# A two-block transformer kernel: one activation table set for Exp and Ln, new rates for the modulation halves, head-norm squares in bursts of four

## The chip, the cores and the metric

The kernel runs on one core of a Trainium2 chip. The metric is the device time of one execution in microseconds (us), as the median of several runs. The engines are named TensorE (PE, with its weight loads PEld), VectorE (DVE), ScalarE (ACT), GpSimd (POOL) and SyncE (SP, which issues the loads here).

## The reference

Two transformer blocks work on 256 tokens of 2048 features, all in float32. The first mixes with eight stick-breaking heads and eight chunk-band heads; the second is modulated by a vector c and mixes with latent attention and sliding-window heads, then runs a gated feed-forward with a short convolution. Cut to what the change touches:

```python
def stick_breaking_attention(q, k, v):
    z = einsum('bhtd,bhsd->bhts', qb, kb) * scale
    log_stay = where(causal, log_sigmoid(-z), 0.0)
    after = cumsum(log_stay, axis=3, reverse=True) - log_stay
    w = where(causal, exp(log_sigmoid(z) + after), 0.0)
    ...

def chunk_band_attention(q, k, v, q_gain, k_gain, rel_table):
    q = rms_norm(q, q_gain)
    k = rms_norm(k, k_gain)
    ...

def second_block(x, c, w_ada, b_ada, ...):
    c_act = silu(c)
    mod = (c_act @ w_ada + b_ada)            # 2048 x 12288
    sh1, sc1, gt1, sh2, sc2, gt2 = split(mod, 6, axis=-1)
    h = rms_norm_2(x, g_pre_mix) * (1.0 + sc1) + sh1
    ...
```

## The kernel before

Every weight comes in chunks of 128 x 1024 float32 (512 KB). A class `Stream` (from L48) holds the list of chunks and takes each through three stages: its load into one of five `raw` buffers, issued on SyncE (L77); its split into an exact high part `whi` on ScalarE (L93) and a low part `wlo` on VectorE (L94), which runs up to three chunks ahead; and its products on TensorE, three for each run of 128 columns (`wmm`, L216 to L218, with the weights stationary; `xmm`, L233 to L235, with the activations stationary and the tokens on the partitions of the result). One chunk has 24 products of 256 columns or 12 of 512.

Tasks are Python generators. `Stream.tick` moves them on twice a chunk, once before it and once in its middle; what a task yields is the number of ticks until its next piece. So one tick is half a chunk. The order of the instructions on TensorE and SyncE is the order in which the code lists them. On VectorE, ScalarE and GpSimd a scheduler orders them by its own estimates; each engine then executes its queue strictly in that order.

The modulation `c_act @ w_ada` is a matrix-vector product and runs on VectorE. It has 192 halves; each loads 512 KB through the same five `raw` buffers and multiplies them with the replicated c (`crep`) in one instruction with an accumulated sum (`ada_half`, L330). `S.after_chunk = ada_tick` adds a rate to an accumulator after each listed chunk and lists a half whenever it has reached one, as long as fewer than a given number exist; `ada_rate(r, upto)` sets both. The halves have deadlines in the code: 64 of them (shift and scale) before the operand of block 2 is made (`make_u` from `start_u`), 160 before that of the feed-forward, 192 before the down projection.

The order of the work in block 1: 9 chunks of the first gates, 24 chunks of gate tiles (`gate_handler`, Silu on ScalarE), then `chunk_group(0)` and `chunk_group(1)`, each q, k and v of four chunk-band heads in 8 chunks apiece, then 16 chunks of values for the stick heads, then 32 chunks of q and k of the eight stick heads, then the 32 chunks of the output projection (`seq`). After k of a group, `head_norm` (L581) squares q and k of four heads (L590, sixteen instructions, eight between two yields), takes the inverse root and multiplies q and k (L599). After v, four `chunk_head` tasks start 1, 6, 11 and 16 ticks later: transposes, `qkT` on ScalarE, scores (L627, L628), a softmax with Exp, transposes to `pT`, products with v (L395, L396). A `stick_head` (L660) multiplies q and k by the tokens' factor into `qkT` on VectorE (L663), starts its scores two ticks later (L666), applies Abs, Exp and Ln on ScalarE (L205 is the line of every ScalarE activation except the split), adds them into `sp` on VectorE (L677), sums over keys on TensorE, and takes another Exp.

In block 2, sliding-window heads and latent heads use Exp, their gates Tanh; the feed-forward uses Silu. A compiler pass places a load of an activation table set in front of an activation whose function the loaded set lacks.

Of the kernel before, what the change touches and what calls it, by code (L numbers as in the profile page):

```python
# [12 lines left out]
AF = mybir.ActivationFunctionType  # L13
ALU = mybir.AluOpType

P = 128
T = 256
# [7 lines left out]
# columns of the packed vectors  # L25
# [9 lines left out]
# columns of the packed constants  # L35
# [12 lines left out]
class Stream:  # L48
    """The order of the work. Weight chunks go through three stages: their load, their split into exact high
    and low float32r parts, and their products; the first two run ahead of the third. Between the products  # L50
    of a chunk, tasks (generators that give the ticks to their next piece) are moved on."""

    RAW, AHEAD = (5,3)
# [9 lines left out]
    # -- the list of work  # L63
# [7 lines left out]
    # -- stages  # L71
# [27 lines left out]
    def split_ahead(self):  # L99
        """split until AHEAD chunks after the running one are ready"""  # L100
        w = sum(1 for i in range(self.nrun, self.nsplit) if self.items[i][0] == "w")
        while self.nsplit < len(self.items) and (w < self.AHEAD + 1 or self.items[self.nsplit][0] == "v"):
            if self.items[self.nsplit][0] == "w":
                w += 1
            self.split_one()

    def run(self):
        """runs every item listed so far"""
        while self.nrun < len(self.items):
            i = self.nrun  # L110
            if self.items[i][0] == "v":
                if self.nsplit <= i:
                    self.split_one()
                self.nrun += 1
                continue
            _, src, n, mms, pre, post = self.items[i]
            if pre is not None:
                pre()
            self.tick()
            self.split_ahead()  # L120
            hi, lo = self.parts.pop(i)
            fs = mms(hi, lo)
            h = (len(fs) + 1) // 2
            for f in fs[:h]:
                f()
            self.tick()
            for f in fs[h:]:
                f()
            self.nrun += 1
            if post is not None:  # L130
                post()

    # -- tasks
# [27 lines left out]
def two_blocks(ctx, tc, xT, cvec, cst, vecs, w1, wo1, bch, ada, wz, wv, wuq, wuk, wuv, bsw, wo2, wup, wup3, wdn, out):  # L161
# [42 lines left out]
    def act(**kw):  # L204
        nc.scalar.activation(**kw)  # L205
# [7 lines left out]
    def wmm(out, whi, wlo, a, first, last):  # L213
        """feature-major: out[feature, token] += W^T a"""
        ahi, alo = a
        mm(out, lhsT=whi, rhs=ahi, start=first, stop=False)  # L216
        mm(out, lhsT=whi, rhs=alo, start=False, stop=False)  # L217
        mm(out, lhsT=wlo, rhs=ahi, start=False, stop=last)  # L218

    def wchunk(lst):  # L220
        """lst: for each run of 128 columns: (out, operand, first, last), values or functions"""
        def mms(hi, lo):
            def one(c, e):
                out, a, first, last = e() if callable(e) else e
                wmm(out, hi[:, c * P:(c + 1) * P], lo[:, c * P:(c + 1) * P], a, first, last)
            return [lambda c=c, e=e: one(c, e) for c, e in enumerate(lst)]
        return mms

    def xmm(hi, lo, j, width, act2, out, b, first, last):
        """token-major: out += a^T W for a block of tokens"""  # L230
        w, t = slice(j * width, (j + 1) * width), slice(b * P, (b + 1) * P)
        ahi, alo = act2
        mm(out, lhsT=ahi[:, t], rhs=hi[:, w], start=first, stop=False)  # L233
        mm(out, lhsT=ahi[:, t], rhs=lo[:, w], start=False, stop=False)  # L234
        mm(out, lhsT=alo[:, t], rhs=hi[:, w], start=False, stop=last)  # L235

# [14 lines left out]
    def rsqrt_cols(v, n):  # L251
        """the same for a few single columns, 1/sqrt(v) / RS: y <- (v y^2 - 3 c^2) y leaves a factor -2 c^2 a step"""
        y = small.tile([P, 2], F32, tag="rz", name="rz", bufs=3)
        a = small.tile([P, 2], F32, tag="rb", name="rb", bufs=2)
        ts(out=y[:, :n].bitcast(I32), in0=v[:, :n].bitcast(I32), scalar1=-0.5, scalar2=1597463007.0, op0=ALU.mult,
           op1=ALU.add)
        for three in (3.0, 12.0, 768.0):
            for c in range(n):
                c1 = slice(c, c + 1)
                stt(out=a[:, c1], in0=y[:, c1], scalar=y[:, c1], in1=v[:, c1], op0=ALU.mult, op1=ALU.mult)  # L260
            for c in range(n):
                c1 = slice(c, c + 1)
                stt(out=y[:, c1], in0=a[:, c1], scalar=three, in1=y[:, c1], op0=ALU.subtract, op1=ALU.mult)
        return y[:, :n]

    def token_rstd(sqs, n):
        """sqs: tiles [P, 2, T] whose sum over tiles, halves and partitions is the sum of squares of each token;
        its mean's 1/sqrt, times 1 / RS"""
# [10 lines left out]
    def replicate(r, dst, gap=3, scale=RS):  # L279
        """dst[p, t] = scale * r of token t"""  # L280
# [17 lines left out]
    class SumSq:  # L298
        """running sum of squares over tiles [P, 2, T]; the last one stays apart"""
# [49 lines left out]
    def ada_rate(r, upto):  # L349
        """halves for each chunk from here on"""  # L350
        ada_acc[1:] = [r, upto]
    S.after_chunk = ada_tick

    # ---- softmax of scores in PSUM [P, 384]: 128 queries x 128 keys, 128 queries x 256 keys; the scores and
    # the biases come negated, so that the least is the negated maximum ----
# [42 lines left out]
    # =========================== block 1 ===========================  # L398
# [43 lines left out]
    def w_pair(srcs, acts, handler, n=16, per=8, tag="g"):  # L442
        """two tiles of 128 features share a bank; handler(bank) follows"""
# [27 lines left out]
    def x_group(srcs, acts, handler, tot, width, tag="g", apart=None):  # L471
        """width features of both blocks of tokens; handler(banks) follows. With apart, the first block is
        finished two chunks before the second, and apart(b, bank) follows each"""
# [42 lines left out]
    def gate_handler(j):  # L516
# [3 lines left out]
        def evac(ps):  # L520
            gt = p1.tile([P, 2, T], F32, tag="gate", name="gate", bufs=8)
            tt(out=gt, in0=two(ps), in1=rrep2, op=ALU.mult)
            act(out=gt, in_=gt, func=AF.Silu)
# [4 lines left out]
    # the first four tiles of gates go by k tiles, behind the split of x  # L528
# [21 lines left out]
    for j in range(2, 8):  # L550
        if j == 2:
            ada_rate(0.3, 96)
        w_pair(next_w1(4), hxs, gate_handler(j))
# [14 lines left out]
    # chunk-band heads  # L568
# [12 lines left out]
    def head_norm(qk, keys):  # L581
        """q, k of four heads, tokens on the partitions: times rsqrt of their mean squares"""
        ss = small.tile([P, 16], F32, tag="sst", name="sst", bufs=2)
        junk = p1.tile([P, 128], F32, tag="junk", name="junk", bufs=1)
        for w in range(2):
# [5 lines left out]
            yield 1  # L591
# [3 lines left out]
        for w in range(2):  # L595
# [4 lines left out]
            yield 1  # L600
# [51 lines left out]
    ada_rate(0.7, 96)  # L652
# [5 lines left out]
    # stick-breaking heads: scores with the keys on the partitions  # L658
# [36 lines left out]
    ada_rate(0.3, 96)  # L695
# [7 lines left out]
    # startup: the first chunks run behind the split of x  # L703
# [15 lines left out]
    # output projection; the residual; the next block's operand without its token factor  # L719
# [6 lines left out]
    def start_u():  # L726
        """room for x * gain, and the shift's columns beside it"""
# [40 lines left out]
    ada_rate(0.5, 96)  # L768
    for n, (j, a, hf) in enumerate(seq):
        if n == 20:  # L770
            ada_rate(0.0, 96)
# [11 lines left out]
    # =========================== block 2 ===========================  # L783
    def trick(srcs, tags, done):
        """some tiles of 128 features from the operand without its token factor: a few k tiles to a chunk"""
# [12 lines left out]
    def untrick(ps, dst, rr):  # L798
        """the token factor and the shift"""
# [7 lines left out]
    def form_h(pool_h, tmp, lst, rr, ish, nb, then=None):  # L807
        """x -> rms(x) * g * (1 + sc) + sh as high and low parts"""
# [38 lines left out]
    def split_q(src, sp=None, bufs=4):  # L847
        """two heads of 64 -> for each its high and low part, on the two halves of the partitions"""
# [60 lines left out]
    ada_rate(0.44, 160)  # L909
# [64 lines left out]
    # latents  # L974
# [71 lines left out]
    # latent attention, two heads at a time  # L1046
# [69 lines left out]
    ada_rate(0.2, 160)  # L1116
# [7 lines left out]
    # output projection, post-norm, gate, residual  # L1124
# [11 lines left out]
    def o_handler(j, a):  # L1136
        """squares and a copy of a pair of tiles; of the last pair each tile by itself"""
# [30 lines left out]
    # =========================== feed-forward ===========================  # L1168
# [35 lines left out]
    def conv_gate(i, z1, z2):  # L1204
        """the two halves of u before the convolution -> high and low parts of silu(u1) * u2"""
# [81 lines left out]
    # down projection: tokens on the partitions, as the output has them  # L1287
# [8 lines left out]
    def to_rows():  # L1296
        """gains along the free dimension, and x with tokens on the partitions"""
# [24 lines left out]
    def finish_block(b, ps):  # L1322
        """the last features, post-norm and residual of a block of tokens"""
# [32 lines left out]
# ---------------------------------------------------------------------------  # L1356
def _wunits(w, cols):
    """w [K, N] -> [len(cols), 128, K/128 * 128]: one unit for each run of 128 columns starting at cols"""
# [14 lines left out]
def _chunks(u):  # L1373
    """[U, 128, n * 1024] -> [U * n, 128, 1024]"""
# [4 lines left out]
def _several(w, cols):  # L1379
    """runs of 128 columns side by side, a few k tiles to a chunk"""  # L1380
# [117 lines left out]
```

## Time and profile before

| | before |
|---|---|
| median of 3 runs | 1987.45 us |
| lowest, highest run | 1982.82, 1987.96 us |
| span of the profiled execution, first to last instruction | 1973.9 us |
| own time of the profiled execution | not given apart from its span |
| TensorE matmul busy | 1912.1 us, 97% |
| TensorE weight load busy | 1792.9 us, 91% |
| VectorE busy | 1373.1 us, 70% |
| ScalarE busy | 1003.2 us, 51% |
| GpSimd busy | 255.7 us, 13% |
| read from HBM | 434.73 MB, 221 GB/s over the span |

The span leaves out what lies before the first and after the last instruction. Busy shares are averages over stages with different limits, so the views that matter are those of single stretches.

### The profile page before, as it was taken

What the parts mean: (1) busy time and instruction counts of PE and PEld (TensorE: products, weight loads), DVE (VectorE), ACT (ScalarE), POOL (GpSimd) and SP (SyncE); (2) the same over time, 40 slices, a digit from 0 to 9 for tenths busy, and PEclk for the clock granted to TensorE, in tenths of its full rate; (3) what the DMA queues carried; (4) which work ended last, traced back from release to release, by engine and by line L of the source; (5) the groups of instructions that cost most, each with busy time, mean ns of one, the idle gap of its engine ahead of it and who ended that gap; (6) DMA issues with size and microseconds to landing.
All of it is one profiled execution on the core that took longest, in us unless ns stands there. A gap on an engine that the chain in (4) does not pass through costs nothing. (4 is left out here: it accounts for less than half of the span.)

```text
span 1973.9 us, 35197 instructions
## 1 busy us (share of the span) xinstructions
PE 1912.1 (97%) x13844; PEld 1792.9 (91%) x13844; DVE 1373.1 (70%) x2204; ACT 1003.2 (51%) x1547; POOL 255.7 (13%) x327
## 2 busy tenths in 40 slices
PE   8998999999999999999999997999999999999997
PEld 7986878999998999999998997999999999988885
DVE  7667776666786666666778889987777766634444
ACT  6434544664465555554566444755455555444432
POOL 2001120000114333331022313100000000000000
PEclk9999999999999999999999998999999999999998
DMA  8788886566666666666555793677777655545553
GB/s 288 258 276 298 269 283 232 199 214 224 222 211 234 226 224 229 230 225 224 192 172 198 268 326 109 218 265 235 235 248 243 224 183 190 182 171 188 186 191 107
DMA packets 128327, 439.14 MB, mean 222 GB/s; under 512 B 14368, under 2 KB 19616, under 8 KB 127904
## 3 DMA queue, kind: packets, MB, share of 16 engines
q1 hardware_dynamic: 128160, 436.89, 65.4%
q8 instruction: 108, 1.77, 0.4%
q14 instruction: 59, 0.48, 0.1%
HBM read 434.73 MB, written 2.10 MB: 221 GB/s over the span
## 5 line engine op out<-in xcount | busy, mean ns | idle before, releaser
L94 DVE TENSOR_TENSOR wlo<-raw,whi 128x1024 fp32r<-128x1024 f32 (+2 forms) x627 | 765.5, 1227 | 290.4 <-ACT whi L93 288.1
L93 ACT ACTIVATE whi<-raw 128x1024 fp32r<-128x1024 f32 (+2 forms) x627 | 650.8, 1042 | 622.9 <-PE g L217 257.3
L216 PE MATMUL g<-h,whi 128*128 128x256 f32 x2064 | 586.7, 284 | 0.2 <-DVE col L802 0.2
L218 PE MATMUL g<-h,wlo 128*128 128x256 f32 x2064 | 580.3, 281 | 0.4 <-DVE wlo L94 0.4
L217 PE MATMUL g<-h,whi 128*128 128x256 f32 x2064 | 580.6, 281 | 0.0
L216 PEld LDWEIGHTS g<-h,whi 128*128 128x128 f32 x2064 | 389.5, 189 | 5.4 <-issue 5.4
L218 PEld LDWEIGHTS g<-h,wlo 128*128 128x128 f32 x2064 | 389.8, 189 | 0.6 <-DVE wlo L94 0.6
L217 PEld LDWEIGHTS g<-h,whi 128*128 128x128 f32 x2064 | 389.7, 189 | 0.0
L330 DVE SCALAR_TENSOR_TENSOR raw<-raw,crep 128x1024 f32<-128x1024 f32 x192 | 240.6, 1253 | 182.8 <-DMA raw<-in_ada_dram 181.2
L216 PE MATMUL g<-hx,whi 128*128 128x256 f32 x448 | 128.4, 287 | 0.0
L218 PE MATMUL g<-hx,wlo 128*128 128x256 f32 x448 | 126.7, 283 | 0.9 <-DVE wlo L94 0.9
L217 PE MATMUL g<-hx,whi 128*128 128x256 f32 x448 | 126.5, 282 | 0.0
L381 POOL TENSOR_TENSOR e<-e,st 128x128 f32<-128x128 f32 x112 | 88.7, 812 | 146.9 <-DVE st L377 139.5
L233 PE MATMUL g<-whi,hx 128*128 128x512 f32 x256 | 105.4, 412 | 0.9 <-ACT v L205 0.9
L234 PE MATMUL g<-wlo,hx 128*128 128x512 f32 x256 | 102.2, 399 | 2.4 <-DVE wlo L94 2.3
L235 PE MATMUL g<-whi,hx 128*128 128x512 f32 x256 | 101.5, 397 | 0.0
L1340 POOL TENSOR_TENSOR y<-y,xt 128x512 f32<-128x512 f32 x2 | 3.2, 1613 | 713.0 <-ACT y L205 713.0
L218 PEld LDWEIGHTS g<-hx,wlo 128*128 128x128 f32 x448 | 85.1, 190 | 1.1 <-DVE wlo L94 1.1
L216 PEld LDWEIGHTS g<-hx,whi 128*128 128x128 f32 x448 | 85.3, 190 | 0.1
L217 PEld LDWEIGHTS g<-hx,whi 128*128 128x128 f32 x448 | 85.2, 190 | 0.1
L205 ACT ACTIVATE e<-e,st 128x128 f32<-128x128 f32 x112 | 50.2, 449 | 56.4 <-DVE st L366 54.6
L218 PE MATMUL g<-mx,wlo 128*128 128x256 f32 x256 | 72.7, 284 | 1.5 <-DVE wlo L94 1.5
(326 smaller groups left out, 3719.3 us busy)
## 6 DMA issues: line engine op xcount, KB each, us to landing
raw<-in_ada_dram SPq DMA_DIRECT2D x192, 512.0 KB, 4.4
raw<-in_wup_dram SPq DMA_DIRECT2D x164, 512.0 KB, 4.1
raw<-in_w_dram SPq DMA_DIRECT2D x127, 512.0 KB, 4.5
raw<-in_wz_dram SPq DMA_DIRECT2D x122, 512.0 KB, 3.7
raw<-in_wdn_dram SPq DMA_DIRECT2D x88, 512.0 KB, 3.2
raw<-in_wo_dram SPq DMA_DIRECT2D x64, 512.0 KB, 4.3
raw<-in_wuq_dram SPq DMA_DIRECT2D x24, 384.0 KB, 3.0
raw<-in_wup_dram SPq DMA_DIRECT2D x16, 384.0 KB, 3.0
```

The source lines that it names most:

```text
L93: nc.scalar.activation(out=hi[:, :n], in_=raw, func=AF.Copy)
L94: nc.vector.tensor_tensor(out=lo[:, :n], in0=raw, in1=hi[:, :n].bitcast(F32), op=ALU.subtract)
L205: nc.scalar.activation(**kw)
L216: mm(out, lhsT=whi, rhs=ahi, start=first, stop=False)
L217: mm(out, lhsT=whi, rhs=alo, start=False, stop=False)
L218: mm(out, lhsT=wlo, rhs=ahi, start=False, stop=last)
L233: mm(out, lhsT=ahi[:, t], rhs=hi[:, w], start=first, stop=False)
L234: mm(out, lhsT=ahi[:, t], rhs=lo[:, w], start=False, stop=False)
L235: mm(out, lhsT=alo[:, t], rhs=hi[:, w], start=False, stop=last)
L330: stt(out=raw, in0=raw, scalar=1.0, in1=crep_now[0][:, h * 1024:(h + 1) * 1024], op0=ALU.mult, op1=ALU.mult, accum_out=modh[:, k:k + 1])
L381: nc.gpsimd.tensor_tensor(out=es, in0=es, in1=st[:, 6 + c:7 + c].to_broadcast([P, w]), op=ALU.mult)
L1340: nc.gpsimd.tensor_tensor(out=t, in0=t, in1=xt[:, b, cols], op=ALU.add)
```

## The change

Three things change in the code; the removed comments and docstrings that the diff also has do nothing.

First, `act` returns its instruction, and behind the Silu of the last gate tile (j = 7) the ScalarE queue gets an instruction that loads the table set `natural_log_exp_and_others`.

Second, the rates of the modulation halves: 0.52 a chunk up to 64 from the third gate tile to the sixth chunk of the output projection, in place of 0.3, 0.7, 0.3 and 0.5 up to 96 by stage; then 0.5 up to 160 to the twentieth chunk; 0.5 in place of 0.44 in block 2's projections; 0.35 in place of 0.2 at the latent heads. The rate 1.0 at the second output projection and 0.3 in the feed-forward stay.

Third, in `head_norm` the two `yield 1` behind eight squares and behind two products move one loop further in, so that they come after four squares and after one product.

```diff
     def act(**kw):
-        nc.scalar.activation(**kw)
+        return nc.scalar.activation(**kw)
...
-            act(out=gt, in_=gt, func=AF.Silu)
+            last = act(out=gt, in_=gt, func=AF.Silu)
+            if j == 7:
+                with tc.issue_after(last.ins):
+                    nc.scalar.preload_act_table_set("natural_log_exp_and_others")
...
         if j == 2:
-            ada_rate(0.3, 96)
+            ada_rate(0.52, 64)
...
     def head_norm(qk, keys):
         for w in range(2):
             for b in range(2):
                 for h in range(4):
                     ...
                     stt(out=junk, in0=q1, scalar=1.0, in1=q1, op0=ALU.mult, op1=ALU.mult, accum_out=ss[:, i:i + 1])
-            yield 1
+                yield 1
...
                 tt(out=q4, in0=q4, in1=r[:, i:i + 4].unsqueeze(2).to_broadcast([P, 4, 128]), op=ALU.mult)
-            yield 1
+                yield 1
...
-    ada_rate(0.7, 96)
     chunk_group(0)
...
     last_head = []
-    ada_rate(0.3, 96)
     for h in range(8):
...
-    ada_rate(0.5, 96)
     for n, (j, a, hf) in enumerate(seq):
+        if n == 6:
+            ada_rate(0.5, 160)
         if n == 20:
-            ada_rate(0.0, 96)
+            ada_rate(0.0, 160)
...
-    ada_rate(0.44, 160)
+    ada_rate(0.5, 160)
     x_group(lambda c: wv[c], hzs, v_handler, 16, 256, tag="t")
...
-    ada_rate(0.2, 160)
+    ada_rate(0.35, 160)
     for pr in range(8):
```

## Rows read from the trace of the kernel before

**Rows 1.** The page's first line: span, instructions.
```profile
span 1973.9 us, 35197 instructions
```

**Rows 2.** Table by stretch: busy us (xinstructions) by engine, granted clock, DMA share, GB/s.
```profile
50.00:97.00 47.00, 47.00 (x400) 47.00 (x399) 28.79 (x34) 20.90 (x23) 0.00 (x0) 1.00 0.78 257
97.00:178.00 81.00, 78.61 (x372) 62.96 (x371) 60.71 (x111) 31.01 (x32) 1.89 (x3) 1.00 0.82 275
178.00:300.00 122.00, 115.37 (x528) 92.64 (x527) 93.26 (x189) 62.43 (x108) 25.34 (x37) 0.99 0.82 282
300.00:420.00 120.00, 116.82 (x885) 112.68 (x884) 76.34 (x101) 70.01 (x84) 0.00 (x0) 0.99 0.64 214
...
950.00:1075.00 125.00, 124.04 (x911) 117.30 (x911) 99.94 (x220) 78.78 (x167) 26.64 (x36) 1.00 0.54 177
1075.00:1180.00 105.00, 100.94 (x820) 99.37 (x820) 87.41 (x130) 45.12 (x69) 26.17 (x18) 0.98 0.84 293
```

**Rows 3.** TensorE's waits, 125 to 350 us: total us, times, longest us.
```profile
PE s L666 <- DVE qkT L663: 3.2, 1, 3.2
PE o L395 <- ACT pT L205: 2.9, 3, 1.5
PE s L627 <- ACT qkT L205: 2.7, 1, 2.7
```

**Rows 4.** VectorE's waits, 50 to 97, 97 to 178, 178 to 300, 300 to 420.
```profile
DVE raw L330 <- DMA raw<-in_ada_dram: 6.2, 4, 2.2
...
DVE raw L330 <- DMA raw<-in_ada_dram: 21.1, 15, 2.2
...
DVE raw L330 <- DMA raw<-in_ada_dram: 22.0, 18, 3.5
...
DVE raw L330 <- DMA raw<-in_ada_dram: 21.6, 8, 4.1
...
DVE sp L677 <- ACT e L205: 5.4, 5, 1.6
```

**Rows 5.** VectorE in order of time: start, duration, instruction, wait before it in brackets.
```profile
124.80 1.23 DVE L330 SCALAR_TENSOR_TENSOR raw<-raw,crep 128x1024 f32<-128x1024 f32 x1 [1.61 <-DMA raw<-in_ada_dram]
...
125.95 1.22 DVE L94 TENSOR_TENSOR wlo<-raw,whi 128x1024 fp32r<-128x1024 f32 x1
```

**Rows 6.** The first chunk-band head, ScalarE and TensorE; then a stretch's table row.
```profile
182.70 1.06 ACT L93 ACTIVATE whi<-raw 128x1024 fp32r<-128x1024 f32 x1 [2.73 <-DMA raw<-in_w_dram]
...
184.54 0.49 PE L627 MATMUL s<-qkT 128*128 128x128 f32 x2 [2.74 <-ACT qkT L205]
...
185.00:188.40 3.40, 3.40 (x10) 2.65 (x9) 3.20 (x9) 2.70 (x6) 0.20 (x1) 0.50 0.99 371
```

**Rows 7.** Table by stretch of line L330 alone: VectorE busy (xinstructions), clock, DMA.
```profile
97.00:178.00 81.00, 22.18 (x36) 1.00 0.82 275
178.00:300.00 122.00, 32.67 (x52) 0.99 0.82 282
300.00:420.00 120.00, 14.79 (x24) 0.99 0.64 214
```

**Rows 8.** VectorE in order of time at the second stick head.
```profile
342.46 1.22 DVE L330 SCALAR_TENSOR_TENSOR raw<-raw,crep 128x1024 f32<-128x1024 f32 x1 [3.90 <-DMA raw<-in_ada_dram]
...
343.62 0.68 DVE L663 TENSOR_TENSOR qkT<-g,rrep 128x512 f32<-128x512 f32 x1
```

**Rows 9.** TensorE in order of time, end of the second output projection.
```profile
1181.79 0.38 PE L218 MATMUL s<-mix,wlo 128*128 128x256 f32 x1 [0.82 <-DVE wlo L94]
```

**Rows 10.** Table loads (group: busy us, mean ns, idle before); ScalarE at the first Tanh.
```profile
L205 ACT ACT_TABLE_LOAD x20 | 25.7, 1283 | 1.1 <-PEq L1488 0.7
...
573.83 0.84 ACT L205 ACTIVATE kd<-z 64x256 fp32r<-64x256 f32 x2
574.70 0.42 ACT L205 ACTIVATE ta<-ta 128x256 f32<-128x256 f32 x1
```

**Rows 11.** ScalarE's waits, 97 to 178 us, behind head_norm's squares.
```profile
ACT whi L93 <- DVE junk L590: 5.2, 2, 3.2
```

## Prediction

> **What bounds the kernel now.** I read the page's first section, then TensorE's waits, then a table by stretch, then VectorE's waits in those stretches, then the order of single instructions. The span is 1973.9 us [rows 1]; the runs' median is 1987.45 us. The page gives no other time for the profiled execution, so I take the 13.55 us between the two as what lies around the span (launch, end, and the scatter of the runs, whose lowest is 1982.82) and add it unchanged to every sum below.
>
> TensorE is the bound: in most stretches it never pauses. From 50 to 97 us (the gate tiles) it is busy 47.00 of 47.00 us; from 97 to 178 (q, k and v of the first chunk-band group) 78.61 of 81; from 178 to 300 (the chunk-band heads) 115.37 of 122; from 300 to 420 (mostly the stick heads) 116.82 of 120 [rows 2]. Only those idle sums, 2.39, 6.63 and 3.18 us, can be won by early modulation work. Their largest pieces are three kinds of waits: 3.2 us for qkT from VectorE, 2.9 us in three waits for pT and 2.7 us for qkT from ScalarE [rows 3].
>
> Behind them stands VectorE. The modulation half (L330) is executed in VectorE's queue in order and waits there for its own 512 KB load. From 97 to 178 us these waits are 21.1 us in 15 times [rows 4]; with 60.71 us of work [rows 2] that is 81.8 of 81 us: VectorE is full though it looks 75% busy. From 178 to 300 it is 93.26 + 22.0 = 115.3 of 122. At 124.80 us one such half starts after 1.61 us of waiting, and the wlo behind it starts the moment it ends, with no wait of its own [rows 5]: the wlo stood behind another tile's load. A late wlo frees its raw buffer late, so the next load is issued late: at 182.70 us ScalarE has waited 2.73 us for raw data, the head's qkT is queued behind that split, and TensorE starts the first scores at 184.54 us after 2.74 us of idling. From 185.0 to 188.4 us the granted clock is 0.50, the 1.2 GHz level [rows 6]; 3.4 us at half speed is 1.7 us of TensorE work lost.
>
> **The change, part by part.**
>
> *Paced halves.* A half is listed after a chunk whenever the rate has summed to one. By the code, the gates' 24 chunks get 12 instead of 7, the 64 chunks of the chunk-band and last value groups 33 instead of 44, the 32 stick chunks 17 instead of 10. At the end of block 1 both have 71. Block 2's projections get 57 for 50, the latent heads 14 for 8, the second output projection 18 for 31. The bytes stay; each moved half moves its load on SP's queue, among the weight loads and the heads' bias loads that use the same queue, and its L330 on VectorE. GpSimd gets nothing.
>
> Gates: a half costs 1.23 us (22.18 us for 18, the x36 counts each with its accumulator read [rows 7]) and waits 21.1/18 = 1.17, so 2.40. TensorE ran 400 products at 24 a chunk in 47 us, thus 16.7 chunks, 2.82 us each. 0.22 more a chunk is 3.7 halves, 8.8 us. VectorE now needs 28.79 + 6.2 = 35.0 us [rows 2, 4]; 43.8 of 47 still fits. I take 0; without that cover each missing microsecond is one of TensorE.
>
> 97 to 178 us: 18 halves become 13.4 (0.52/0.7), 4.6 x 2.40 = 11.1 us less, 70.7 of 81. 178 to 300: 26 halves [rows 7] at 32.67/26 = 1.26 us and 22.0/26 = 0.85 us of waiting; 6.7 fewer take 14 us away, 101 of 122. So the starvation should end, and with it the late raw data, the first head's stall and its slow clock. At stake are 2.39 + 6.63 + 1.7 = 10.7 us; I leave 1.0 us for one of the three pT waits. **-9.7 us**, bounds 0 and -10.7.
>
> 300 to 420 us: 12 halves become 17.7 here, at 14.79/12 + 21.6/12 = 3.03 us each: +17.3 us, against 76.34 + 21.6 + 5.4 now (the 5.4 is VectorE waiting for the Ln results [rows 4], which goes). 115 of 120 fits, but tightly, and single waits hurt: at 342.46 us a half had waited 3.90 us, qkT came right after it [rows 8], and TensorE lost 3.2 us; it also shows 0.99 as mean clock [rows 2], like the stretch before, so I charge another 1.7. That one event is 4.9 us for 12 halves. Scaled by 17.7/12 it is 7.2: **+2.3 us**, bounds -4.9 (no head is caught) and, with all eight heads caught, 7 x 4.9 = +34.
>
> Second output projection: it ends at 31 halves now, and TensorE idles 4.06 us from 1075 to 1180 [rows 2] plus 0.82 us at 1181.79 [rows 9]. With 18 the halves end 14 chunks earlier; most of the idle time there belongs to the latent heads' tails. **-1.0**, bounds 0 and -4.9. Latent heads: 0.96 us idle at 8 halves [rows 2]; 14 of them, by proportion, **+0.7**, bounds 0 and +4.1 (the denser stretch). Projections in between: 7 halves over 114 chunks, 0. Start: the first half is listed two chunks earlier and needs the replicated c; one more 1.23 us ahead of a wlo at worst, **+0.3**, bounds 0 and +1.2.
>
> *Table set.* 20 loads of 1283 ns [rows 10]; 16 alternate between Exp and Ln in the eight stick heads. One set holding both would take some 15 x 1.283 = 19 us off ScalarE. No wait of TensorE in rows 3 stands behind a load, and ScalarE is busy 70.01 of 120 us there [rows 2]: 0 on the path, only the 5.4 us of VectorE above. The preload itself sits behind the last gate's Silu, where 20.90 of 47 us are busy: 0; whi behind it has the lead that TensorE's full 47 us show. But something may come back: the first Tanh, at 574.70 us, follows the kd copy with no load between [rows 10], since the set left by the last Exp serves it. If the new set does not, one load of 1.283 us delays the split behind it. **+0.3**, bounds 0 and +1.3.
> The Trainium skill (ScalarE: Activation LUTs, Table sets: the hidden batching unit) lists tanh with exp_and_others and names only exp and ln for natural_log_exp_and_others. The trace agrees on the first half. By the same page (What ACT_TABLE_LOAD costs) a switch is about 2.66 us with its drain; with that price the upper bound here would be +2.7 instead of +1.3.
>
> *Bursts of four.* head_norm takes 9 resumptions instead of 5; they begin one tick after k's last chunk, the first head 17 ticks after it, a tick being half a chunk, 1.41 us. It ends 6 to 7 ticks early, so 0; each missing tick would cost 1.41 us in that head. ScalarE waited 5.2 us, twice, behind these squares [rows 11]; shorter bursts can give back part, but only inside the starvation already counted: 0.
>
> Sum: -9.7 + 2.3 - 1.0 + 0.7 + 0.3 + 0.3 = **-7.1 us**. 1973.9 - 7.1 = 1966.8 us of span, +13.55 = 1980.3; I say **1980 us**.
>
> **The rivals.**
> A, *better*: the stick stall goes as well, since Ln no longer holds VectorE up and the order shifts: -9.7 - 4.9 - 1.0 + 1.3 = -14.3, 1973 us. For it: a single head of eight was caught. Against: more halves there, 3.03 us each.
> B, *the waits stay*: a half waits because VectorE meets it before its load has landed; with the denser gates the ring of raw buffers may already be short at 97 us, and half of the 9.7 stays. -7.1 + 4.9 = -2.2, 1985 us. For it: the halves wait from 50 to 97 us too, 6.2 us, at less than half the rate [rows 4].
> C, *slower*: in the stick stretch the halves catch qkT often. A head hands qkT to its scores within two ticks, 2.8 us, and a wait of 3.90 us exceeds that. Each caught head costs 4.9 us. Three caught heads (two more than now, 9.8 us) eat the 9.4 us of the other terms; from five the result is slower: -9.4 + 4 x 4.9 = +10.2, 1998 us. For it: eight waits of 2.7 us on average, 4.1 at most, in this stretch; against: only one of them met a qkT.
> D, *the table set is not kept*: if loads are chosen by function, the 16 stay. The path does not change: 1980 us, less 0.3 for Tanh.
>
> **How the numbers follow.** Forecast 0.50, with a range of its own from 1974 to 1985; A 0.12, B 0.18, C 0.13, D 0.07. A difference under 0.3%, 6.0 us, is about what a measurement of this kernel cannot tell from none: faster is below 1981.5, slower above 1993.4. Below 1981.5 lie 0.37 of the forecast, A, and 0.05 of D: 0.54. Slower is C: 0.13. The rest, 0.33, is the same. The range of 8 in 10 reaches from 1969 (A with the second projection's bound) to 1993, which leaves out C.
>
> **What would show it.** Right: TensorE busy without a pause from 97 to 178 us, no wait for qkT at the first head, no half clock near 185 us; VectorE's waits for L330 below 15 us in that stretch; about five table loads, one ahead of the first Tanh. Wrong: wlo waits of TensorE that begin before 140 us (B); several waits of about 3 us for qkT at the stick heads, with the half clock behind them (C); 20 loads (D); late halves that stall the latent heads by over 3 us. What could break the sum is that the order of VectorE's and ScalarE's queues is not written out, so every stretch may shift by a stall or two.

## The result, and the profile after

| | before | after |
|---|---|---|
| median | 1985.78 us (4 runs, 1982.82 to 1987.96) | 2009.39 us (4 runs, 2005.24 to 2014.91) |
| after / before, 95% interval | | **1.0132 [1.0111, 1.0154]** |
| span of the profiled execution | 1973.9 us | 2013.1 us |

The change makes the kernel 1.3% slower. The forecast was 1980 us, a small gain, and the range ended at 1993. The two spans lie 39.2 us apart, the medians 23.6. The profiled execution of after took 2014.91 us, the slowest of its runs and 1.8 us more than its span; so hardly anything lies around a span, and the profile of before shows an execution some 10 us faster than its median. Differences between these two traces are therefore somewhat too large, and the experiments below are needed for sizes.

The page of after: its first lines, and its chain of work that ended last (shares of the span by engine, then by line); below it the chain of before, by engine.
```profile
span 2013.1 us, 35174 instructions
...
PE 1924.4 (96%) x13844; PEld 1797.5 (89%) x13844; DVE 1363.9 (68%) x2204; ACT 978.3 (49%) x1532; POOL 247.7 (12%) x327
...
PE 27%; DMA 4%; DVE 3%; issue 1%; DVEq 0%; ACT 0%
PE g L218 5%; PE g L217 5%; PE g L216 5%; DMA raw<-in_ada_dram 4%; PE g L235 2%; PE g L234 2%; PE g L233 2%; PE s L234 2%; PE s L235 2%; PE s L233 2%; DVE wlo L94 2%; PE s L216 0%; PE s L217 0%; PE s L218 0%; DVE u L1214 0%
```
```profile
PE 36%; DVE 1%; DVEq 0%; ACT 0%; issue 0%
```
VectorE and ScalarE do no more work than before. The halves' loads now stand on the chain with 4% of the span, where before has none. But the chain is followed back only to 1288 us in after, and these loads lie between 1421 and 1594 us, in the feed-forward; of the earlier stages it says nothing. The whole span is covered by the groups of the modulation half; first after, then before (xcount | busy, mean ns | idle before it, and what ended most of that).
```profile
L330 DVE SCALAR_TENSOR_TENSOR raw<-raw,crep 128x1024 f32<-128x1024 f32 x192 | 240.0, 1250 | 276.2 <-DMA raw<-in_ada_dram 275.8
```
```profile
L330 DVE SCALAR_TENSOR_TENSOR raw<-raw,crep 128x1024 f32<-128x1024 f32 x192 | 240.6, 1253 | 182.8 <-DMA raw<-in_ada_dram 181.2
```
The same 192 halves, at the same 1.25 us each, wait 276 us for their loads instead of 182. These waits are VectorE's idle time, so its busy share even fell, from 70% to 68%.

Where the time came, by stage. Each stage is cut at the start of the first product of a chunk of the list, so that both kernels have the same TensorE work in it; lengths in us, and in brackets the halves executed there and their waits for loads.

| stage | before | after | after, order (see below) |
|---|---|---|---|
| chunk-band groups and heads | 152.7 (33, 29) | 147.4 (25, 29) | 142.9 (25, 0) |
| values for the stick heads | 56.6 (11, 17) | 57.7 (8, 22) | 52.6 (8, 0) |
| stick heads | 110.4 (11, 16) | 122.9 (17, 22) | 105.4 (16, 0) |
| output projection, first projections of block 2 | 147.0 (10, 14) | 144.5 (11, 9) | 143.1 (11, 0) |
| sliding-window heads and projections | 380.3 (48, 31) | 397.0 (55, 100) | 373.4 (55, 0) |
| latent heads | 129.1 (11, 2) | 138.2 (16, 9) | 130.1 (16, 0) |
| second output projection | 111.2 (27, 11) | 111.1 (14, 7) | 110.3 (15, 0) |
| feed-forward, up | 405.9 (32, 53) | 412.8 (32, 72) | 406.0 (32, 0) |

The start (+0.8) and the down projection (0.0) complete the 39.2. The rows of four of these stages, in the columns of [rows 2]: after, then before.
```profile
106.80:254.20 147.40, 145.36 (x643) 116.80 (x641) 107.89 (x221) 69.23 (x94) 13.18 (x23) 0.99 0.78 259
...
311.90:434.80 122.90, 109.84 (x862) 107.04 (x861) 79.20 (x110) 50.64 (x69) 0.00 (x0) 0.96 0.69 220
...
579.30:976.30 397.00, 382.50 (x3026) 362.39 (x3027) 259.85 (x483) 193.99 (x390) 109.17 (x190) 0.99 0.71 226
976.30:1114.50 138.20, 129.46 (x924) 119.91 (x922) 107.79 (x227) 83.95 (x177) 31.75 (x38) 0.99 0.60 188
```
```profile
106.00:258.70 152.70, 146.64 (x641) 116.07 (x640) 117.64 (x238) 69.15 (x93) 14.43 (x23) 0.99 0.83 280
...
315.30:425.70 110.40, 107.22 (x864) 105.91 (x862) 71.69 (x97) 67.28 (x81) 0.00 (x0) 0.98 0.63 209
...
572.70:953.00 380.30, 375.66 (x3026) 360.25 (x3027) 255.77 (x471) 194.24 (x389) 119.31 (x190) 1.00 0.67 226
953.00:1082.10 129.10, 126.00 (x924) 118.81 (x922) 103.76 (x219) 84.03 (x177) 29.66 (x38) 1.00 0.56 185
```
In the sliding-window stage TensorE, with the same products, idles 14.5 us where it idled 4.6, and VectorE has work for only 259.85 of 397.00 us. The other 6.8 of the 16.7 us lie in TensorE's busy time (382.50 us for 375.66, at a mean granted clock of 0.99 for 1.00); what they are made of was not traced. The idle time of TensorE is spread over many waits. The largest of after, over the whole span (total us, times, longest), and VectorE's wait in the sliding-window stage:
```profile
PE t L388 <- POOL e L381: 18.6, 30, 1.8
PE s L668 <- DVE qkT L665: 11.5, 6, 6.3
PE g L218 <- DVE wlo L94: 9.5, 14, 2.0
PE o L395 <- ACT pT L205: 8.1, 7, 2.0
...
DVE raw L330 <- DMA raw<-in_ada_dram: 100.4, 51, 4.1
```
How a half makes a head late, instruction by instruction (start, duration, instruction, wait before it): the first stick head of after, VectorE and TensorE.
```profile
330.26 1.23 DVE L330 SCALAR_TENSOR_TENSOR raw<-raw,crep 128x1024 f32<-128x1024 f32 x1 [3.67 <-DMA raw<-in_ada_dram]
...
331.41 1.22 DVE L94 TENSOR_TENSOR wlo<-raw,whi 128x1024 fp32r<-128x1024 f32 x1
332.55 0.68 DVE L665 TENSOR_TENSOR qkT<-g,rrep 128x512 f32<-128x512 f32 x1
...
333.29 1.22 PE L668 MATMUL s<-qkT 128*128 128x256 f32 x2 [6.34 <-DVE qkT L665]
```
And the table row, in the columns of [rows 2], of a stretch within and behind that wait:
```profile
328.20:338.40 10.20, 5.11 (x22) 4.93 (x23) 5.80 (x7) 2.13 (x4) 0.00 (x0) 0.50 0.68 235
```
VectorE stands 3.67 us at the half, then a split and only then qkT follow without a pause, and TensorE has idled 6.34 us. The granted clock is 0.50, the 1.2 GHz level, over this whole stretch, which begins within that idle time.

### The profile page after: what moved, and what is told of

It is laid out like the page before. It is cut to its first block, busy times and chain, and to the rows that moved or that the text cites. A ratio compares the mean times of both kernels' runs of the same rounds, so it can differ in the third digit from the quotient of the medians.

```text
span 2013.1 us, 35174 instructions
## 1 busy us (share of the span) xinstructions
PE 1924.4 (96%) x13844; PEld 1797.5 (89%) x13844; DVE 1363.9 (68%) x2204; ACT 978.3 (49%) x1532; POOL 247.7 (12%) x327
## 5 line engine op out<-in xcount | busy, mean ns | idle before, releaser
L94 DVE TENSOR_TENSOR wlo<-raw,whi 128x1024 fp32r<-128x1024 f32 (+2 forms) x627 | 759.4, 1219 | 253.1 <-ACT whi L93 250.0
L330 DVE SCALAR_TENSOR_TENSOR raw<-raw,crep 128x1024 f32<-128x1024 f32 x192 | 240.0, 1250 | 276.2 <-DMA raw<-in_ada_dram 275.8
L381 POOL TENSOR_TENSOR e<-e,st 128x128 f32<-128x128 f32 x112 | 81.1, 743 | 168.4 <-DVE st L377 158.3
```

The source lines that it names most:

```text
L94: nc.vector.tensor_tensor(out=lo[:, :n], in0=raw, in1=hi[:, :n].bitcast(F32), op=ALU.subtract)
L330: stt(out=raw, in0=raw, scalar=1.0, in1=crep_now[0][:, h * 1024:(h + 1) * 1024], op0=ALU.mult, op1=ALU.mult, accum_out=modh[:, k:k + 1])
L381: nc.gpsimd.tensor_tensor(out=es, in0=es, in1=st[:, 6 + c:7 + c].to_broadcast([P, w]), op=ALU.mult)
```

## The experiments

Each kernel was timed beside runs of before on the same chip. The median of before differed between these sets (1975.12, 1976.07, 1980.42 and 1978.33 us), so only the ratio within a set is used. First the parts, one at a time.

**The table set alone** (`act` returns its instruction, and the preload behind the last gate's Silu).
```diff
...
+            if j == 7:
+                with tc.issue_after(last.ins):
+                    nc.scalar.preload_act_table_set("natural_log_exp_and_others")
```


> The kernel before with the table set alone. Theory 1 (block 2's denser halves block VectorE's queue): within 4 us of the kernel before, five table loads in place of 20, and no wait of TensorE changes by over 3 us in any stretch. Theory 2 (the stick heads' denser halves do it): the same. Theory 3 (the changed table set reorders the queues of ScalarE and VectorE): at least 8 us slower, with new waits for qkT at the stick heads.

Measured 1975.56 us, ratio 1.0007 [0.9984, 1.0030]: nothing, with 5 loads in place of 20.

**Bursts of four alone** (the two `yield 1` one loop further in; the diff shows one of them).
```diff
-            yield 1
+                yield 1
```


> The kernel before with the bursts of four alone. All theories: within 4 us of the kernel before. If the scheduler's order reacts to any edit, waits move by some us in stretches after 250 us although the edit ends there.

Measured 1976.43 us, ratio 1.0000 [0.9975, 1.0026]: nothing.

**The rates of block 1 alone.**
```diff
-            ada_rate(0.3, 96)
+            ada_rate(0.52, 64)
...
-    ada_rate(0.7, 96)
...
-    ada_rate(0.3, 96)
...
-    ada_rate(0.5, 96)
...
+        if n == 6:
+            ada_rate(0.5, 160)
...
```


> The kernel before with the new rates of block 1 alone (0.52 up to 64, then 0.5). Theory 1: between 2 us faster and 7 us slower: some 5 us won from 97 to 300 us, about 9 us lost in waits for qkT at the stick heads, nothing from 600 us on. Theory 2: 15 to 24 us slower, nearly the whole difference. Theory 3: no slower than the kernel before.

Measured 1983.27 us, ratio 1.0036 [1.0016, 1.0056]: slower. Its stage of chunk-band heads took 144.8 us, its stick heads 123.2. The sliding-window stage, whose rate and 48 halves are those of before, took 386.1 with 62 us of waits instead of 31: the halves fall on other chunks there, since the accumulator arrives with another remainder. TensorE's wait at its stick heads:
```profile
PE s L665 <- DVE qkT L662: 12.6, 6, 6.0
```

**The rates of block 2 alone.**
```diff
-    ada_rate(0.44, 160)
+    ada_rate(0.5, 160)
...
-    ada_rate(0.2, 160)
+    ada_rate(0.35, 160)
```


> The kernel before with the new rates of block 2 alone (0.5 and 0.35). Theory 1: 15 to 25 us slower; VectorE's waits for the halves' loads from 600 to 940 us grow from 27 us to over 80 us, and TensorE waits for the softmax rows (L388) at most sliding-window heads. Theory 2 and theory 3: within 4 us of the kernel before.

Measured 1998.92 us, ratio 1.0112 [1.0071, 1.0153]. Sliding-window stage 393.0 us, latent heads 138.3. This is most of the loss, in the two stages that the prediction had charged with 0 and +0.7.

**Only 0.5 for 0.44, then 0.48.** At 0.5 a half falls behind every second chunk; a rival reading was that this fixed step locks the halves onto one place in the heads' rhythm.
```diff
-    ada_rate(0.44, 160)
+    ada_rate(0.5, 160)     # second kernel: 0.48
```


> The kernel before with 0.5 in place of 0.44 in block 2's projections alone. If the sliding-window stretch's waits carry the larger part: 9 to 16 us slower than the kernel before, the latent heads' stretch as before, halves waiting over 70 us in the sliding-window stretch. If the latent heads' 0.35 carries it: under 5 us slower.

> The kernel before with 0.48 in place of 0.44 in block 2's projections. Density theory (each further half costs its wait): 55 of the 114 chunks' halves instead of 50, so 5 of the 7 that 0.5 adds: about 70% of the cost of 0.5, 7 to 11 us slower. Lock theory (at 0.5 a head pair's six chunks hold exactly three halves, which fall on the same place in each pair): within 4 us of the kernel before, halves waiting under 45 us in that stretch.

Measured 1991.08 us, ratio 1.0076 [1.0061, 1.0091], and 1987.77 us, 1.0060 [1.0044, 1.0077], a little more than the 7 to 11 us expected of 0.48. Five of the seven added halves cost 11.7 of the 15.0 us of the whole time, so no lock at 0.5 is needed: that is 2.1 and 2.3 us for each added half. In the two traces the sliding-window stage itself takes 391.7 and 386.7 us, 11.4 and 6.4 more than in before. That the count of halves alone sets this is not shown: with the rates of block 1 alone the old 48 halves, on other chunks, already took 386.1 us there.

**The halves do not wait.** In the changed kernel the half multiplies crep alone and no longer reads what it loads, so the modulation's sums are left out. All loads stay, and so does VectorE's work in total.
```diff
-            stt(out=raw, in0=raw, scalar=1.0, in1=crep_now[0][:, h * 1024:(h + 1) * 1024], op0=ALU.mult, op1=ALU.mult,
+            c_ = crep_now[0][:, h * 1024:(h + 1) * 1024]
+            stt(out=c_, in0=c_, scalar=0.0, in1=crep_now[0][:, h * 1024:(h + 1) * 1024], op0=ALU.mult, op1=ALU.mult,
```


> The changed kernel; the halves' multiplication reads the replicated c alone and not its loaded tile, so the modulation's sums are left out (zero), while all loads and all of VectorE's work stay. Theory of the in-order wait (VectorE stands at a half until its load lands, and what it owes TensorE stands behind it): at least 20 us faster than the changed kernel, so below the kernel before or equal to it; no waits of VectorE for halves' loads; the waits for qkT at stick heads and for the softmax rows mostly gone. Theory of plain load (too much work on VectorE, or too much traffic, in those stretches): within 8 us of the changed kernel.

Measured 1957.78 us, ratio 0.9911 [0.9896, 0.9926]: 2.2% faster than after (0.9911 / 1.0132) with the same loads and in total nearly the same VectorE work. The half's group:
```profile
L331 DVE SCALAR_TENSOR_TENSOR crep<-crep 128x1024 f32<-128x1024 f32 x192 | 233.2, 1227 | 0.4 <-ACT crep L205 0.4
```
But the work does not stay in its place. A half that needs no load can run at any time, and the scheduler put 161 of the 192 ahead of 427.5 us. The sliding-window stage has none of them: its row in the columns of [rows 2], then line L331 alone in the columns of [rows 7].
```profile
570.60:944.50 373.90, 373.66 (x3029) 358.60 (x3028) 192.97 (x363) 190.57 (x381) 92.71 (x190) 1.00 0.72 240
```
```profile
570.60:944.50 373.90, 0.00 (x0) 1.00 0.72 240
```
So this run shows that the traffic doesn't carry the loss: 54 halves are loaded in this stage, and it takes 373.9 us. Waits and work of the halves are both gone from it, and which of them costs is left to the next experiment. The crowding shows in the chunk-band stage, which takes 159.1 us here; the largest wait of TensorE lies there, for a step of a head (qt) that VectorE now does late:
```profile
PE t L625 <- DVE qt L603: 10.5, 2, 6.2
```

**The order.** If what hurts is that VectorE meets a half before its load has landed, it is enough to put the half later in VectorE's queue: behind the low part (L94) of the split that the code listed last before it.
```diff
-            nc.vector.tensor_tensor(out=lo[:, :n], in0=raw, in1=hi[:, :n].bitcast(F32), op=ALU.subtract)
+            self.last_lo = nc.vector.tensor_tensor(out=lo[:, :n], in0=raw, in1=hi[:, :n].bitcast(F32), op=ALU.subtract)
...
-            stt(out=raw, in0=raw, scalar=1.0, in1=crep_now[0][:, h * 1024:(h + 1) * 1024], op0=ALU.mult, op1=ALU.mult,
-                accum_out=modh[:, k:k + 1])
+            with tc.issue_after(S.last_lo.ins):
+                stt(out=raw, in0=raw, scalar=1.0, in1=crep_now[0][:, h * 1024:(h + 1) * 1024], op0=ALU.mult, op1=ALU.mult,
+                    accum_out=modh[:, k:k + 1])
```
In the changed kernel:

> The changed kernel with each half's multiplication queued on VectorE behind the low-part split that was listed before it, so that the scheduler can't put it ahead. If the order that the scheduler chose is the cause: 8 to 20 us faster than the changed kernel, and the halves' waits for loads fall below half of the changed kernel's. If a half meets its load too early in any order: within 5 us of the changed kernel.

Measured 1947.42 us, ratio 0.9860 [0.9843, 0.9876]: 2.7% faster than after (0.9860 / 1.0132), some 54 us where 8 to 20 were expected. The half's group:
```profile
L331 DVE SCALAR_TENSOR_TENSOR raw<-raw,crep 128x1024 f32<-128x1024 f32 x192 | 240.8, 1254 | 0.5 <-ACT crep L205 0.4
```
VectorE in order of time, in a sliding-window head; the half starts without a wait behind the split:
```profile
746.49 1.23 DVE L94 TENSOR_TENSOR wlo<-raw,whi 128x1024 fp32r<-128x1024 f32 x1 [1.62 <-ACT whi L93]
747.64 1.22 DVE L331 SCALAR_TENSOR_TENSOR raw<-raw,crep 128x1024 f32<-128x1024 f32 x1
```
And the table rows of stick heads and sliding-window stage:
```profile
301.70:407.10 105.40, 105.40 (x862) 104.32 (x861) 77.29 (x106) 51.17 (x68) 0.00 (x0) 1.00 0.76 246
...
550.20:923.60 373.40, 373.40 (x3029) 358.59 (x3028) 257.54 (x483) 194.10 (x386) 111.82 (x190) 1.00 0.74 239
```
275.8 us of waits are gone with one edit that removes no work. TensorE is busy for the whole of both stages, with 16 and 55 halves executed in them (after has 17 and 55). VectorE's work in the sliding-window stage is that of after, 257.54 us for 259.85: so the waits carry the loss, and not the work. Not every wait costs, though: the feed-forward takes 406.0 us without any and took 405.9 in before with 53 us of them.

In the kernel before, and in the changed kernel with the old rates of block 2 (0.44 and 0.2) or one of them (0.5 and 0.2):

> The kernel before with the order alone: each half's multiplication queued behind the low-part split listed before it. If the scheduler's place for the halves is the cause in the kernel before too: 15 to 25 us faster than the kernel before, without any wait of VectorE for a half's load; from 97 to 178 us TensorE still may wait for wlo, since 0.7 halves a chunk load 318 GB/s by the code at 2.82 us a chunk. If the new rates are what makes the order pay: within 8 us of the kernel before.

> The changed kernel with the order, and with block 2's rates as before (0.44, 0.2). If the rates of block 2 cost only through the waits that the order takes away: within 3 us of the changed kernel with the order (1947 us). If the denser halves of the latent heads load VectorE by themselves: 3 to 8 us faster than that, won from 950 to 1100 us, part of it given back in the second output projection, whose halves become 31 again.

> The changed kernel with the order, with 0.5 in the projections as changed and 0.2 at the latent heads as before. By the stretches read so far the latent heads' 0.35 costs some 4 us there even without waits for loads: 2 to 6 us faster than the changed kernel with the order, and the sliding-window stretch as long as there (373 us).

Measured 1947.29 us, 0.9841 [0.9822, 0.9859]; 1948.02, 0.9843 [0.9827, 0.9858]; 1948.46, 0.9844 [0.9828, 0.9859]. With the order the rates, the table set and the bursts make no difference that these runs can tell. The four medians lie within 1.2 us of each other, 1.4 to 1.6% below before; this is the version to keep, with either set of rates. The 2 to 6 us that 0.2 at the latent heads was expected to bring did not come.

**GpSimd's queue.** The trace of after shows the same kind of wait on another engine: in a sliding-window head GpSimd waits for the 64 KB load of the next head's bias table, and this head's sum st stands behind it.
```profile
790.01 1.23 DVE L330 SCALAR_TENSOR_TENSOR raw<-raw,crep 128x1024 f32<-128x1024 f32 x1 [4.08 <-DMA raw<-in_ada_dram]
...
790.20 1.43 POOL L929 TENSOR_SCALAR tab<-tab 128x128 f32<-128x128 f32 x1 [8.87 <-DMA tab<-in_bsw_dram]
...
791.16 1.30 DVE L94 TENSOR_TENSOR wlo<-raw,whi 128x1024 fp32r<-128x1024 f32 x1
...
792.83 0.19 POOL L375 TENSOR_TENSOR st<-st 128x2 f32<-128x2 f32 x1
...
793.06 0.17 DVE L377 RECIPROCAL st<-st 128x2 f32<-128x2 f32 x1 [0.59 <-POOL st L375]
...
793.37 1.85 POOL L381 TENSOR_TENSOR e<-e,st 128x128 f32<-128x128 f32 x2 [0.34 <-DVE st L377]
...
794.70 0.33 PE L388 MATMUL t<-cs,e 128*128 128x128 f32 x1 [1.83 <-POOL e L381]
```
Read alone, this head blames GpSimd: VectorE is through with half and split at 792.46 us and then waits 0.59 us for GpSimd's sum. And the order edit on VectorE also changed GpSimd's order, since the scheduler places anew: in that kernel the sum comes ahead of the table. So one more kernel: the changed one with the bias operations queued behind the sum, the halves left alone.
```diff
-            nc.gpsimd.tensor_tensor(out=st[:, 2:4], in0=st[:, 2:4], in1=st[:, 4:6], op=ALU.add)
+            lst = nc.gpsimd.tensor_tensor(out=st[:, 2:4], in0=st[:, 2:4], in1=st[:, 4:6], op=ALU.add)
+            if late:
+                with tc.issue_after(lst.ins):
+                    late()
...
-            load_tab(h + 1)
+            late = load_tab(h + 1)      # issues the load; its three bias operations come by late()
```


> The changed kernel, in which GpSimd's three bias operations of a sliding-window head (fed by the 64 KB load of tab) are queued behind that head's sum st on GpSimd; the modulation halves keep their place. In the changed kernel GpSimd waits 196.0 us in 29 times for tab, and the sum of the head before it stands behind 28 of them; VectorE waits 100.4 us for the halves' loads in that stretch. If VectorE's waits carry the loss of the sliding-window stretch, this brings little: the stretch stays within 5 us of the changed kernel's 397.0, and the time stays 0.9% to 1.3% above before. If the late link is GpSimd's order, the stretch falls to 375 to 381 us with VectorE's waits still near 100, and the time comes to about 0.1% to 0.5% above before.

Measured 1997.68 us, ratio 1.0104 [1.0069, 1.0139]. Its sliding-window stage, the table row:
```profile
572.00:965.50 393.50, 381.86 (x3027) 362.97 (x3028) 258.51 (x484) 195.47 (x390) 108.97 (x190) 0.99 0.70 228
```
GpSimd's wait for the table and VectorE's for the halves in it:
```profile
POOL tab L936 <- DMA tab<-in_bsw_dram: 5.2, 10, 1.1
...
DVE raw L330 <- DMA raw<-in_ada_dram: 112.1, 49, 3.9
```
GpSimd's wait falls from 196.0 to 5.2 us, and the stage from 397.0 to only 393.5. The other way round, in the kernel whose halves do not wait (and lie outside this stage) GpSimd still waits 188.9 us for tables, and the stage takes 373.9 us. So GpSimd's waits alone delay nothing, and VectorE's make the heads late. At most the 3.5 us came back with GpSimd's, and the kernels at 0.5 without the order differ by as much without that edit (391.7 to 397.0 us).

## Why the prediction was wrong

**The mechanism was seen, but not priced everywhere.** The prediction read from [rows 4, 5] that the half waits in VectorE's queue and that a split stands behind it. It then charged this wait as if it were work (2.40 or 3.03 us a half), asked whether work and waits together still fit the stretch, and found room. But the loss doesn't begin when VectorE is full. One half that VectorE meets 4 us early delays whatever stands next in the queue by 4 us, in a stretch where VectorE works 65% of the time. The Trainium skill (PSUM — Partial Sum Buffer, Engine vs sequencer instructions) calls the queues of ScalarE, VectorE and GpSimd strict FIFO; the trace agrees, with the 4.08 us in which VectorE starts nothing ahead of the half at 790.01 us.

**The step that failed: "Projections in between: 7 halves over 114 chunks, 0."** It was measured at +16.7 us in the trace; 0.5 for 0.44 alone cost 15.0 us of the whole time, some 2.1 us for each of 7 halves (11.4 us in this stage of its trace). No row of this stretch backs the 0: the prediction's rows stop at 420 us and begin again at 950, apart from the first Tanh. VectorE's wait for halves there, 30.9 us in 29 times in before, was in the trace and went to 100.4 us in 51; so it wasn't only the 7 new halves that waited, but nearly all of the 55. TensorE's wait behind GpSimd's e (L388), the largest there, went from 4.2 us in 2 times to 12.2 in 24.

**Latent heads: +0.7, bound +4.1; measured +9.1.** The proportion was taken from TensorE's idle time in before, 0.96 us, at a low density at which VectorE waited for halves only 4 times, 1.6 us in all; and the window ended at 1075 us, while the stage goes on to 1082.1 and idles 3.1. The stall of over 3 us that the forecast named as a sign came. Block 2's rates alone give the same 138.3 us.

**Stick heads: +2.3; measured +12.5.** Rival C had the mechanism and the place: a half catches qkT, and the clock falls behind it. It priced a caught head at 4.9 us throughout. One head cost far more (6.3 us of waiting and, at 5.11 us of work in 10.20, some 2.5 us of half clock), the other five waited 5.2 us together, 1.0 each. What made the kernel slower beyond this stage came from the two stages above, which no rival named.

**Chunk-band heads: -9.7; measured -5.3 between the traces, and about -4.** The 152.7 of before's trace is a high value. In the five other kernels with the old rate and without the order this stage took 148.4 to 150.8 us; the three traces with the new rate and without the order have 144.8, 145.9 and 147.4. The means, 150.2 of all six and 146.0, are 4.2 us apart. One half of the reading held: from 97 to 178 us the lower density did end TensorE's idling, busy 80.89 of 81 us where it was 78.61. From 178 to 300 us it did not (117.12 of 122, for 115.37), and more of that stretch ran at the lower clock. In the columns of [rows 2], after:
```profile
97.00:178.00 81.00, 80.89 (x391) 66.41 (x390) 59.08 (x106) 36.44 (x39) 1.40 (x3) 1.00 0.83 273
178.00:300.00 122.00, 117.12 (x533) 94.80 (x532) 83.95 (x175) 59.37 (x104) 25.23 (x37) 0.97 0.75 252
```
At the first chunk head the wait for qkT fell from the 2.74 us of [rows 6] only to 1.93, and the granted clock is again 0.50 behind it:
```profile
188.01 0.65 PE L630 MATMUL s<-qkT 128*128 128x128 f32 x2 [1.93 <-ACT qkT L205]
```
```profile
188.20:191.60 3.40, 3.40 (x10) 2.74 (x10) 3.26 (x8) 1.16 (x4) 0.00 (x0) 0.50 0.66 242
```
The forecast's sign "VectorE's waits for L330 below 15 us from 97 to 178 us" failed: 19.3 us in 10 times where there were 21.1 in 15: fewer waits, and longer ones. That was rival B's reading. Density is not the full cure here: with the order alone, and the old rate of 0.7, the stage takes 143.3 us, since the extra halves fit once none of them waits.

**The base.** The 13.55 us "around the span" do not exist. With the 1.8 us measured in after, the profiled execution of before took some 1976 us, so the sum should have been set against a median known to lie above the profile. The sign of the forecast doesn't hang on this, but it makes every later comparison of the two traces too large.

**Right steps.** The gates have room for more halves (TensorE busy 47.00 of 47 us at 0.52, as at 0.3). The second output projection kept its length with 13 fewer halves; of the -1.0 only 0.1 came. The bursts cost and gave nothing. The table set took 15 loads off ScalarE with no effect on the time, and the load ahead of the first Tanh came, as forecast. The group of the loads (the fifth is the preload), then ScalarE at the first Tanh:
```profile
L205 ACT ACT_TABLE_LOAD x4 | 5.1, 1283 | 0.8 <-PEq L1490 0.7
```
```profile
581.28 1.28 ACT L205 ACT_TABLE_LOAD   x1
582.58 0.42 ACT L205 ACTIVATE ta<-ta 128x256 f32<-128x256 f32 x1
```
ScalarE goes on 0.02 us after the 1.28 us load. The Trainium skill (ScalarE: Activation LUTs, What ACT_TABLE_LOAD costs) gives some 2.66 us with a drain; this trace shows 1.30 us from the load's start to the next activation, and the added load agrees with its Table sets section, which lists tanh with exp_and_others.

**Left open.** The feed-forward, at an unchanged 0.3, took 6.9 us longer, with 72 us of waits for 53. But the changed kernel with GpSimd's edit took 406.0 us there, as before, with 50 us of waits, and the kernels with one part of the change each took 404.5 to 408.8. VectorE's waits there differ from program to program (45 to 72 us); why after got long ones wasn't separated. What decides which half lands ahead of which step was not traced either, only that it disappears with the queue position.

## What to carry to other kernels

An instruction that waits for a DMA in an in-order queue holds up everything behind it; read busy time and head-of-queue waits together, per stage, and ask for each such instruction what stands next in its queue. Where a scheduler places it by its estimates, fix its place behind work that will be late anyway, before tuning how often it comes: here the rates alone moved the time by up to 1.1% for the worse, and the position brought it 1.4 to 1.6% below before at any rate tried. And a stage whose density the change alters is never costed at 0 without a row of its own.

## What the runs showed that was not expected

- Denser loads are harmless by themselves. With the order, the sliding-window stage reads at 239 GB/s, faster than before's 226, with TensorE busy for all of it.
- A late half holds its buffer. SyncE issues loads in order and waits for a free raw buffer: in the sliding-window stage its wait for a half that frees one was 75.6 us before, 134.1 after and 32.4 with the order. Its wait for splits went the other way (154.8, 103.6 and 189.8 us), so the sum hardly moved, and that this delays later loads is not shown.
- Within one TensorE pause of 6.34 us the granted clock fell to 0.50, and it stayed there until 338.4 us, 5.1 us after work had begun again; the order left no pause in that stage, and its mean granted clock is 1.00 where after's is 0.96.
- An edit on one engine changed another engine's order: with the halves fixed on VectorE, GpSimd's wait for the bias tables fell from 196.0 to 35.1 us without being touched.
- An experiment that takes a dependence away also sets the scheduler free: the halves that need no load went to other stages, so their stages lost the work together with the wait. Fixing the place kept the work where it was.
